# Hybrid attention block: second score pass on half the array's rows for two heads at once, and two pieces of elementwise work issued later

## Chip, cores and metric

One NeuronCore of one Trainium2 chip runs the whole program in one launch. The metric is device time in microseconds (us); the figure before is the median of three runs. TensorE (PE) multiplies matrices, and its weight loads are listed apart as PEld. VectorE is DVE, ScalarE is ACT, GpSimd is POOL, and SyncE (SP) issues the DMAs.

## The reference, cut to what matters

The block has 1024 tokens of width 1024. A gated linear recurrence and a sparse attention run on the same normed input, are merged by gates, and a squared-ReLU MLP follows. The parts that matter here:

```python
qg = q.reshape(...) * (HD ** -0.5)                # 8 heads of 64, in 2 groups of 4
p_s = masked_softmax(einsum('bghqd,bgqkd->bghqk', qb, k_sel), tok_ok)      # selected branch
p_w = masked_softmax(einsum('bghqd,bgkd->bghqk', qb, k_w), m_w)            # window branch
...
hn = rmsnorm(h, norm2_g[l])
h = h + jnp.square(jax.nn.relu(hn @ w_ff1[l])) @ w_ff2[l]
return rmsnorm(h, final_g)
```

With 1024 tokens the selection takes every causal block, so the selected branch is plain causal attention over all keys up to the query. The window branch sees the last 512 keys. A block of 128 queries is called `qb` (0 to 7), a group of four heads `g`.

## The kernel before, in words

**Precision.** Every fp32 matrix is split into a high part (rounded to the engine's fp32r format) and a low rest; a product of two such matrices is three matmuls (high-high, high-low, low-high; `mm3`, L241). For the attention scores the split is laid along the rows instead: a head has 64 channels, so the 128 rows of the array hold q-high in rows 0 to 63 and q-low in rows 64 to 127 (`split_q` L799, transposed into `qS`). The keys in `kS` hold, for x=0, k-high twice (once for each half of the rows) and, for x=1, k-low twice. So one head's scores are two matmuls over all 128 rows (L894): first pass (q-high + q-low) times k-high, second pass (q-high + q-low) times k-low. A mask is added in PSUM by a bf16 matmul of the identity with a 128x128 mask tile (L897): `diag` on the query's own block, `far` on the block four back in the window branch.

**Scores.** `scores(qb, g)` (L851) is a generator that issues one chunk between two `yield`s. A chunk is one PSUM tile of 1024 columns from `psA` (two buffers of two banks). For qb below 4 the tile holds two heads of up to 512 columns (`pair = 2`), for qb 4 to 7 one head of up to 1024 columns. Keys are taken in two halves of 512, because an output lies in one bank. After the matmuls DVE takes the row maximum (L901), ACT the exponential (L910), and after all four heads of a branch DVE the reciprocal (L915) and POOL the scaling (L919).

**Attention.** `attend()` (L1001) walks a list of steps, one for each key block of each branch of each unit (qb, g): four transposes of probabilities on PE into a `psB` bank (L934), a high copy on ACT (L936), a low rest on DVE (L937), and three steps later two matmuls with the values (L1045). Between steps it draws chunks of the scores of the next unit, spread evenly over the steps of the present one (`n_all`, L1020: eight chunks, four where qb is below 4, and one more for the compressed branch when g is 0). The compressed branch's steps have 63 keys, so their two value matmuls use 63 of the array's rows (`vcS`). The tile framework adds the waits and may place an instruction before an earlier one on its engine.

**Second norm.** In the second half of the tokens (th=1), after each of four output tiles j of the merge projection is added to the residual (L1399), the generator `norm2` (L1116) is advanced twice: once for the norm of tile j (h_d DMA, ACT square, POOL power at L249 and L250, DVE scaling at L1122), and once for the tile's sums and differences (L1134 DVE, L1135 POOL, L1136 DVE, L1137 POOL), which the fast (Strassen-like, seven products) MLP needs as operands S1, S2 and S4. After tile 2, `ahead(-1)` prepares the first four MLP weight operands (ACT copy L1185, DVE rest L1186). The MLP's first products P1 need only the first half's A11; S2 and S3 are transposed (L1108, `turned`) after the first and second of them.

**First MLP product.** For each of 16 column pairs p, `f1_prod` (L1203) issues the seven products in the order P1, P6, P7, P2, P5, P4, P3 (12 matmuls each, L1217) into the banks a, c, d, a, e, d, e; c and e are the two halves of one `psA` tile `f1c`. After each product come its sums (`add` is L1221 whatever it adds), ReLU on ACT and square. After P4: `ub[0]` is squared, POOL adds `ud` to it into `ub[1]` (L1253), then DVE subtracts `ua` from `ub[0]` in place (L1254), and a DMA stores `ub`. After P3 the same for `uc` (POOL square L1225, DVE add L1221, DVE L1261, DMA L1262). P6's sum is `u2 = c + p1`, named `u` in the rows. POOL also makes the weight sums `w1t` (L1175) and DVE the rests of the weight operands `w1op` (L1186). On SP's queue the loads of `w1r` (L1167) for p+2 follow the stores of p.

Of the kernel before, what the change touches and what calls it, by code (L numbers as in the profile page):

```python
# [19 lines left out]
D = 1024  # L20
# [5 lines left out]
NH = 8  # L26
# [23 lines left out]
def fb(ap):  # L50
    return ap.bitcast(F32)
# [3 lines left out]
def tile_hybrid_block(ctx, tc, x, positions, norm1_g, w_in, lb_param, hgrn_norm_g, pe_k, pe_v,  # L55
# [733 lines left out]
    def prep(th):  # L789
        qt = QT[th]  # L790
        qS[th] = [a8("qS") for _ in range(2)]
        kS[th] = [a8("kS") for _ in range(2)]
        tmp = s4(name="rtmp")
        for i in range(2):
            rope2(qt[i].rearrange("p t (h d) -> p t h d", h=NH), th, i, NH, tmp[:, i * 256:256 + i * 256])
            yield 1300.0 * th
        QX = {}

        def split_q(h2):  # L799
            qx = QX[h2] = s4(F32R, name="qx").rearrange("p (h t x d) -> p h t x d", h=2, t=4, x=2)  # L800
            for i in range(2):
                src = qt[i].rearrange("p t (h d) -> p h t d", h=NH)[:, h2:h2 + 2]
                hi = qx[:, :, 2 * i:2 * i + 2, 0, :]
                nc.scalar.copy(hi, src)
                nc.vector.tensor_tensor(qx[:, :, 2 * i:2 * i + 2, 1, :], src, fb(hi), op=OP.subtract)

        for br in range(2):
            for g in range(2):
                kx = KXS.pop((th, br, g))
                for x_ in range(2):  # L810
                    pt = psB("ptk")
                    for j in range(4):
                        nc.tensor.transpose(pt[:, j * 128:(j + 1) * 128],
                                            kx[:, j, x_].rearrange("p e d -> p (e d)"), ident)
                    dst = kS[th][br][:, g * 2 + x_, :]
                    if x_:
                        nc.scalar.copy(dst, pt)
                    else:
                        nc.vector.tensor_copy(dst, pt)
                if br:  # L820
                    split_q(g * 2)
                yield 800.0
        for h2 in range(0, NH, 2):
            qx = QX.pop(h2)
            for e in range(2):
                h = h2 + e
                pt = psB("ptq")
                for j in range(4):
                    nc.tensor.transpose(pt[:, j * 128:(j + 1) * 128],
                                        fb(qx[:, e, j]).rearrange("p x d -> p (x d)"), ident)  # L830
                dst = qS[th][h // 4][:, h % 4, :]
                if h % 2:
                    nc.scalar.mul(dst, pt, 0.125)
                else:
                    nc.vector.tensor_scalar(dst, pt, 0.125, None, op0=OP.mult)
            if h2 + 4 < NH:
                split_q(h2 + 4)
            yield 800.0
        del QT[th]
# [11 lines left out]
    def scores(qb, g):  # L851
# [23 lines left out]
            PC[qb] = Pc  # L875
            yield
        den = small.tile([128, 3, 8], F32, name="den", tag="den", bufs=3)
        pair = 2 if qb < 4 else 1
        for br, kb0 in ((0, 0), (1, k_lo)):
            nk = (qb + 1 - kb0) * 128  # L880
            for h0 in range(0, 4, pair):
                sc = psA("sc")
                for hh in range(h0, h0 + pair):
                    off = (hh - h0) * 512
                    for half in range(2):
                        a, e = max(kb0, half * 4), min(qb + 1, half * 4 + 4)
                        if a >= e:
                            continue
                        cs = slice(off + a * 128, off + e * 128)
                        ks = slice((a % 4) * 128, (a % 4 + e - a) * 128)  # L890
                        masks = [(k, m) for k, m in ((qb, diag), (qb - 4, far))
                                 if a <= k < e and (m is diag or br == 1)]
                        for x_ in range(2):
                            nc.tensor.matmul(sc[:, cs], qS[th][g][:, hh, qsl], kS[half][br][:, g * 2 + x_, ks],  # L894
                                             start=x_ == 0, stop=x_ == 1 and not masks)
                        for mi, (k, m) in enumerate(masks):
                            nc.tensor.matmul(sc[:, off + k * 128:off + (k + 1) * 128], identb, m, start=False,  # L897
                                             stop=mi == len(masks) - 1)
                i0 = br * 4 + h0
                sv = sc.rearrange("p (h k) -> p h k", h=pair)[:, :, kb0 * 128:(qb + 1) * 128]  # L900
                nc.vector.tensor_reduce(den[:, 2, i0:i0 + pair], sv, axis=AX.X, op=OP.max, negate=True)  # L901
                for hh in range(h0, h0 + pair):
                    i = br * 4 + hh
                    if qb < 4:
                        if br == 0:
                            PP[qb, g, 8 + hh] = s4(name="P")
                        PP[qb, g, i] = PP[qb, g, 8 + hh][:, br * 512:br * 512 + nk]
                    else:
                        PP[qb, g, i] = s4(name="P")[:, :nk]
                    nc.scalar.activation(PP[qb, g, i], sv[:, hh - h0], AF.Exp, bias=den[:, 2, i:i + 1],  # L910
                                         accum_out=den[:, 0, i:i + 1])
                if h0 + pair == 4:
                    bs = slice(br * 4, br * 4 + 4)
                    nc.vector.tensor_scalar(den[:, 1, bs], den[:, 0, bs], 1e-30, None, op0=OP.max)
                    nc.vector.reciprocal(den[:, 1, bs], den[:, 1, bs])  # L915
                    for h_ in range(4):
                        i = br * 4 + h_
                        pv_ = PP[qb, g, i]
                        nc.gpsimd.tensor_scalar(pv_, pv_, den[:, 1, i:i + 1],  # L919
                                                gat[:, qb, (g * 4 + h_) * 3 + 1 + br:(g * 4 + h_) * 3 + 2 + br],  # L920
                                                op0=OP.mult, op1=OP.mult)
                yield
# [78 lines left out]
    def attend():  # L1001
# [4 lines left out]
        for si in range(len(steps) + LAG):  # L1006
            if si < len(steps):
                qb, g, br, k, i, n = steps[si]
                u = units.index((qb, g))
                if i == 0 and si:  # L1010
                    for _ in nxt:
                        yield 1300.0
                    if u + 1 < len(units):
# [3 lines left out]
                            W.stop = 10 ** 9  # L1017
                            W.ensure(n_before_merge + 1, 0)
                        nb, ng = units[u + 1]
                        nxt, n_done, n_all = scores(nb, ng), 0, (4 if nb < 4 else 8) + (ng == 0)  # L1020
                    else:
                        nxt = iter(())
                        W.stop, W.load, W.ahead = 10 ** 9, 1, 1
# [90 lines left out]
        nc.vector.tensor_tensor(l, p3, fb(h), op=OP.subtract)  # L1114

    def norm2(th, hs_):  # L1116
        for j in range(4):
            t = th * 4 + j
            nc.sync.dma_start(h_d[t * 128:(t + 1) * 128, :], hs_[j])
            hn = HN[t] = s4(name="hn")  # L1120
            rs = rms_scale(hs_[j], hn, D)
            nc.vector.scalar_tensor_tensor(hn, hs_[j], rs, g2b, op0=OP.mult, op1=OP.mult)  # L1122
            yield 2600.0
            if th == 0:
                for q, nm in enumerate(("A11", "A12")):
                    turned(nm, [HN[x_][:, q * 512:(q + 1) * 512] if x_ == j else None for x_ in range(4)], j)
                yield 1000.0
                continue

            if j % 2 == 0:  # L1130
                HS1.append(s4(name="hs1"))
            a11, a12, a21, a22 = HN[j][:, :512], HN[j][:, 512:], hn[:, :512], hn[:, 512:]
            s1 = HS1[j // 2][:, (j % 2) * 512:(j % 2) * 512 + 512]
            nc.vector.tensor_tensor(s1, a21, a22, op=OP.add)  # L1134
            nc.gpsimd.tensor_tensor(a21, a11, a21, op=OP.subtract)  # L1135
            nc.vector.tensor_tensor(a11, s1, a11, op=OP.subtract)  # L1136
            nc.gpsimd.tensor_tensor(a12, a12, a11, op=OP.subtract)  # L1137
            yield 1000.0

    def turn(nm, banks):  # L1140
        x0, c0 = {"S1": (None, 0), "S2": (0, 0), "S3": (4, 0), "S4": (0, 512), "A22": (4, 512)}[nm]
# [61 lines left out]
    def f1_prod(p, nm):  # L1203
# [44 lines left out]
        elif nm == "P4":  # L1248
# [2 lines left out]
            add(ub[:, 0], ps_["d"], post["u2"])  # L1251
            sq(ub[:, 0], nc.vector)
            nc.gpsimd.tensor_tensor(ub[:, 1], ub[:, 0], ud, op=OP.add)  # L1253
            nc.vector.tensor_tensor(ub[:, 0], ub[:, 0], post["ua"][:, 0], op=OP.subtract)  # L1254
            nc.sync.dma_start(u_d[p][2:4].rearrange("x p c -> p x c"), ub)
        else:
            uc = ring("uc", 2, p).rearrange("p (x c) -> p x c", x=2)
            add(uc[:, 0], ps_["e"], post["u2"])
            sq(uc[:, 0], nc.gpsimd)
            add(uc[:, 1], post["ua"][:, 0], uc[:, 0])  # L1260
            nc.vector.tensor_tensor(uc[:, 0], uc[:, 0], post["ud"], op=OP.subtract)  # L1261
            nc.sync.dma_start(u_d[p][4:6].rearrange("x p c -> p x c"), uc)  # L1262
            del UP[p], PB[p]


# [102 lines left out]
    for th in range(2):  # L1368
# [11 lines left out]
        for dh in range(2):  # L1380
# [8 lines left out]
            for j in range(4):  # L1389
# [10 lines left out]
                if th == 1 and dh == 1:  # L1400
                    next(n21)
                    if j == 2:
                        ahead(-1)
                    next(n21)
                pump(2600)
            del ws
        del M[th]
        if th == 0:
            n2 = spawn(norm2(0, hs_))
        else:  # L1410
            ahead(0)
            hs_ = None
    yb = None
# [62 lines left out]
```

## Time and profile before

| what | value |
|---|---|
| median of 3 runs | 1645.74 us (1644.25 to 1648.33) |
| profiled execution | 1644.42 us, its span 1642.7 us, mean granted clock 0.997 |
| PE busy | 1604.9 us (98%), 8342 matmuls |
| PE weight loads | 1338.5 us (81%) |
| DVE busy | 1033.1 us (63%) |
| ACT busy | 740.9 us (45%) |
| POOL busy | 589.2 us (36%) |

A span is the time from the first to the last instruction. An instruction's busy time runs from its start to its end, and successive matmuls overlap, so "busy" is not a count of useful cycles. Attention lies from about 540 to 870 us of the span, the second norm from 977 to 1006 us, the first MLP product from 993 to about 1320 us.

### The profile page before, as it was taken

Reading aid. Unit: us, or ns where it says so; the run is one execution under the profiler, and the core shown is the slowest. Engines: PE = TensorE matmul, PEld = TensorE weight load, DVE = VectorE, ACT = ScalarE, POOL = GpSimd, SP = SyncE. Lnnn points to the kernel's source line nnn. Section 1 sums busy time; section 2 is a strip of 40 time slices with the busy share of each in tenths; the row PEclk is TensorE's granted clock in tenths of the full one; section 3 lists DMA queues with packets and bytes.
Section 4 is the critical chain, followed back from the end, with each engine's and each line's share of the span. In section 5 each row is a group of like instructions: output and inputs, shape, how many; then the busy total and the mean of one; then the engine's idle time right before and its main releaser. Section 6 shows DMA issues by size and latency. Waiting matters only on the chain. (4 is left out here: it accounts for less than half of the span.)

```text
span 1642.7 us, 22944 instructions
## 1 busy us (share of the span) xinstructions
PE 1604.9 (98%) x8342; PEld 1338.5 (81%) x8342; DVE 1033.1 (63%) x1615; ACT 740.9 (45%) x1422; POOL 589.2 (36%) x587
## 2 busy tenths in 40 slices
PE   8999999999999999999999998999999999999998
PEld 7898897889888888788788876877777788888886
DVE  6464454122537467988886646766666678887766
ACT  5343334220646365877764414333333356334443
POOL 2221222010112363444322135455555422564554
PEclk9999999999999999999999999999999999999999
DMA  5210111232434000000037722444444499888852
GB/s 187 72 43 23 39 39 29 85 107 77 132 107 153 27 1 1 1 1 1 14 118 267 269 85 69 141 148 141 141 141 141 167 324 345 305 301 320 301 182 107
DMA packets 145827, 211.67 MB, mean 129 GB/s; under 512 B 11649, under 2 KB 72241, under 8 KB 145714
## 3 DMA queue, kind: packets, MB, share of 16 engines
q1 hardware_dynamic: 145714, 210.21, 38.0%
q8 instruction: 66, 1.08, 0.3%
q14 instruction: 47, 0.39, 0.1%
HBM read 164.03 MB, written 46.14 MB: 128 GB/s over the span
## 5 line engine op out<-in xcount | busy, mean ns | idle before, releaser
L1305 POOL TENSOR_TENSOR gr<-gw 128x512 f32<-128x512 f32 x80 | 124.2, 1565 | 135.2 <-DMA gw<-in_w_ff_dram 72.6
L155 POOL TENSOR_TENSOR wlo<-wraw,whi 128x1024 fp32r<-128x1024 f32 (+1 forms) x28 | 67.4, 2407 | 274.5 <-ACT whi L152 247.2
L242 PE MATMUL gT<-xh,whi 128*128 128x512 f32 x384 | 152.7, 398 | 0.0
L244 PE MATMUL gT<-xh,wlo 128*128 128x512 f32 x384 | 150.3, 391 | 0.0
L243 PE MATMUL gT<-xl,whi 128*128 128x512 f32 x384 | 150.1, 391 | 0.0
L919 POOL TENSOR_SCALAR P<-P,den,gat 128x640 f32<-128x640 f32 (+7 forms) x128 | 100.1, 797 | 120.2 <-DVE den L915 61.3
L155 DVE TENSOR_TENSOR wlo<-wraw,whi 128x1024 fp32r<-128x1024 f32 (+2 forms) x59 | 81.8, 1394 | 94.0 <-ACT whi L152 89.6
L1217 PE MATMUL f1c<-xoh,w1op 128*128 128x512 f32 x384 | 127.8, 394 | 9.3 <-DVE u L1221 9.3
L1186 DVE TENSOR_TENSOR gu<-gr,gu 128x512 fp32r<-128x512 f32 x112 | 103.5, 924 | 47.2 <-ACT gu L1185 47.1
L1185 ACT CAST gu<-gr 128x512 fp32r<-128x512 f32 x112 | 69.4, 620 | 139.6 <-DVE gx L1186 109.7
L1186 DVE TENSOR_TENSOR gx<-gr,gx 128x512 fp32r<-128x512 f32 x112 | 109.7, 980 | 4.0 <-ACT gx L1185 4.0
L937 DVE TENSOR_TENSOR pth<-pT,pth 128x512 fp32r<-128x512 f32 (+1 forms) x148 | 98.7, 682 | 21.3 <-ACT pth L936 19.9
L910 ACT ACTIVATE P<-sc,den 128x640 f32<-128x640 f32 (+7 forms) x128 | 89.7, 705 | 43.9 <-DVE den L901 38.9
L894 PE MATMUL sc<-kS,qS 128*128 128x512 f32 (+3 forms) x384 | 96.7, 361 | 0.6 <-ACT P L910 0.5
L1045 PE MATMUL oT<-pth,vS 128*128 128x512 f32 x264 | 96.7, 441 | 0.0
L936 ACT CAST pth<-pT 128x512 fp32r<-128x512 f32 (+1 forms) x148 | 85.0, 588 | 23.9 <-PE pT L934 19.8
L1217 PEld LDWEIGHTS f1c<-xoh,w1op 128*128 128x128 f32 x384 | 72.0, 188 | 29.1 <-DVE u L1221 13.2
L901 DVE TENSOR_REDUCE den<-sc 128x1 f32<-128x640 f32 (+7 forms) x96 | 84.5, 883 | 16.7 <-PE sc L897 15.9
L152 ACT CAST whi<-wraw 128x1024 fp32r<-128x1024 f32 (+2 forms) x87 | 88.6, 1039 | 12.6 <-PE po L243 6.1
L1217 PE MATMUL f1a<-xoh,w1op 128*128 128x512 f32 x256 | 86.5, 398 | 1.6 <-DVE w1op L1186 1.6
L243 PE MATMUL gA<-gx,gu 128*128 128x512 f32 x224 | 87.4, 390 | 0.4 <-DVE gx L1186 0.2
L242 PE MATMUL gA<-gx,gu 128*128 128x512 f32 x224 | 87.3, 390 | 0.0
(343 smaller groups left out, 4428.6 us busy)
## 6 DMA issues: line engine op xcount, KB each, us to landing
gw<-in_w_ff_dram SPq DMA_DIRECT2D x160, 256.0 KB, 5.3
gr<-u_d SPq DMA_DIRECT2D x112, 256.0 KB, 5.0
wraw<-in_w_in_dram SPq DMA_DIRECT2D x40, 512.0 KB, 5.4
w1r<-in_w_ff_dram SPq DMA_DIRECT2D x32, 512.0 KB, 4.6
wraw<-in_w_out_dram SPq DMA_DIRECT2D x16, 512.0 KB, 6.8
u_d<-ua SPq DMA_DIRECT2D x16, 512.0 KB, 2.8
u_d<-ub SPq DMA_DIRECT2D x16, 512.0 KB, 2.8
u_d<-uc SPq DMA_DIRECT2D x16, 512.0 KB, 3.1
```

The costliest lines, as they stand in the source:

```text
L155: eng.tensor_tensor(lo, raw, fb(hi), op=OP.subtract)
L242: nc.tensor.matmul(o, l[0], r[0], start=start, stop=False)
L243: nc.tensor.matmul(o, l[0], r[1], start=False, stop=False)
L244: nc.tensor.matmul(o, l[1], r[0], start=False, stop=stop)
L894: nc.tensor.matmul(sc[:, cs], qS[th][g][:, hh, qsl], kS[half][br][:, g * 2 + x_, ks], start=x_ == 0, stop=x_ == 1 and not masks)
L910: nc.scalar.activation(PP[qb, g, i], sv[:, hh - h0], AF.Exp, bias=den[:, 2, i:i + 1], accum_out=den[:, 0, i:i + 1])
L919: nc.gpsimd.tensor_scalar(pv_, pv_, den[:, 1, i:i + 1], gat[:, qb, (g * 4 + h_) * 3 + 1 + br:(g * 4 + h_) * 3 + 2 + br], op0=OP.mult, op1= ...
L937: nc.vector.tensor_tensor(pth[:n, 1], pt[:n], fb(pth[:n, 0]), op=OP.subtract)
L1045: nc.tensor.matmul(oT, vv, pth[:m, x_], start=i == 0 and x_ == 0, stop=i == n - 1 and x_ == 1)
L1186: nc.vector.tensor_tensor(l, src, fb(h), op=OP.subtract)
L1217: nc.tensor.matmul(dst, w_[:, kt, :], x_.kt(kt), start=first and kt == 0 and i == 0, stop=kt == 3 and i == 2, skip_group_check=True)
L1305: nc.gpsimd.tensor_tensor(t0[:, 1], t1[:, 0], t1[:, 1], op=OP.add if GORDER[i][1][2] > 0 else OP.subtract)
```

## The change

Four edits:

1. `split_q` writes, for the odd head of a pair, q-high into rows 64 to 127 and q-low into rows 0 to 63, by four half-size pairs of copy and subtraction instead of two.
2. `scores` handles two heads in every chunk. The first pass is as before. The second pass multiplies only q-high with k-low, on 64 rows: the even head on rows 0 to 63, the odd head on rows 64 to 127, one right after the other, into different banks. For qb 4 to 7 a chunk now takes both `psA` tiles, one for each head. The masks of both heads follow the second pass of the half that they are in. The product of q-low and k-low is left out. `n_all` falls from 8 to 4 chunks for qb 4 to 7.
3. `norm2` for the second half of the tokens is advanced once for each tile j instead of twice: the call issues the differences of tile j-2 (from tile 2 on) and then the norm of tile j. The differences of the last two tiles come after the loop (`drain_gen`), before `ahead(0)`.
4. The subtraction `ub[0] -= ua[0]` and the store of `ub` move from after P4 to after P3, behind the store of `uc`.

```diff
             for i in range(2):
-                src = qt[i].rearrange("p t (h d) -> p h t d", h=NH)[:, h2:h2 + 2]
-                hi = qx[:, :, 2 * i:2 * i + 2, 0, :]
-                nc.scalar.copy(hi, src)
-                nc.vector.tensor_tensor(qx[:, :, 2 * i:2 * i + 2, 1, :], src, fb(hi), op=OP.subtract)
+                for e in range(2):
+                    src = qt[i].rearrange("p t (h d) -> p h t d", h=NH)[:, h2 + e]
+                    hi = qx[:, e, 2 * i:2 * i + 2, e, :]
+                    nc.scalar.copy(hi, src)
+                    nc.vector.tensor_tensor(qx[:, e, 2 * i:2 * i + 2, 1 - e, :], src, fb(hi), op=OP.subtract)
...
-        pair = 2 if qb < 4 else 1
...
+            for h0 in (0, 2):
+                if qb < 4:
+                    sc = psA("sc")
+                    scs = [sc[:, :512], sc[:, 512:]]
+                else:
+                    scs = [psA("sc") for _ in range(2)]
+                for x_ in range(2):
                     for half in range(2):
...
+                        for d_ in range(2):
+                            rows = slice(d_ * 64, d_ * 64 + 64) if x_ else slice(0, 128)
+                            nc.tensor.matmul(scs[d_][:, a * 128:e * 128], qS[th][g][rows, h0 + d_, qsl],
+                                             kS[half][br][rows, g * 2 + x_, ks], start=x_ == 0,
+                                             stop=x_ == 1 and not masks)
+                        for d_ in range(2 if x_ else 0):
+                            for mi, (k, m) in enumerate(masks):
+                                nc.tensor.matmul(scs[d_][:, k * 128:(k + 1) * 128], identb, m, start=False,
+                                                 stop=mi == len(masks) - 1)
...
-                        nxt, n_done, n_all = scores(nb, ng), 0, (4 if nb < 4 else 8) + (ng == 0)
+                        nxt, n_done, n_all = scores(nb, ng), 0, 4 + (ng == 0)
...
     def norm2(th, hs_):
-        for j in range(4):
+        for j in range(5):
+            if j < 4:
...
+                yield 2600.0
...
+            if j == 0:
+                continue
+            i = j - 1
...
             nc.vector.tensor_tensor(s1, a21, a22, op=OP.add)
             nc.gpsimd.tensor_tensor(a21, a11, a21, op=OP.subtract)
             nc.vector.tensor_tensor(a11, s1, a11, op=OP.subtract)
             nc.gpsimd.tensor_tensor(a12, a12, a11, op=OP.subtract)
-            yield 1000.0
...
             nc.gpsimd.tensor_tensor(ub[:, 1], ub[:, 0], ud, op=OP.add)
-            nc.vector.tensor_tensor(ub[:, 0], ub[:, 0], post["ua"][:, 0], op=OP.subtract)
-            nc.sync.dma_start(u_d[p][2:4].rearrange("x p c -> p x c"), ub)
         else:
...
             nc.sync.dma_start(u_d[p][4:6].rearrange("x p c -> p x c"), uc)
+            nc.vector.tensor_tensor(ub[:, 0], ub[:, 0], post["ua"][:, 0], op=OP.subtract)
+            nc.sync.dma_start(u_d[p][2:4].rearrange("x p c -> p x c"), ub)
...
                     if j == 2:
                         ahead(-1)
-                    next(n21)
...
+            drain_gen(n21)
             ahead(0)
```

## Rows read from the trace of the kernel before

**Rows 1.** Busy time by stage, 650 to 700 us; columns as in its first line.
```profile
core 0: us, PE busy (x) PEld busy (x) DVE busy (x) ACT busy (x) POOL busy (x), PEclk, DMA share, GB/s
650.00:700.00 50.00, 49.24 (x326) 38.75 (x324) 45.57 (x84) 39.36 (x93) 21.19 (x26) 1.00 0.00 1
```

**Rows 2.** Waits of PE: who waited for whom, us in total, times, longest.
```profile
PE f1c L1217 <- DVE u L1221: 9.3, 12, 0.9
...
PE pt L1108 <- DVE xol L1114: 3.9, 1, 3.9
...
PE f1a L1217 <- DVE w1op L1186: 1.6, 1, 1.6
```

**Rows 3.** Groups by line and shape, PE, score matmuls: busy us, mean ns of one.
```profile
L894 PE MATMUL sc<-kS,qS 128*128 128x512 f32 x144 | 49.1, 429 | 0.6 <-ACT P L910 0.5
...
L894 PE MATMUL sc<-kS,qS 128*128 128x384 f32 x80 | 22.5, 370 | 0.0
...
L894 PE MATMUL sc<-kS,qS 128*128 128x256 f32 x80 | 17.8, 312 | 0.0
...
L894 PE MATMUL sc<-kS,qS 128*128 128x128 f32 x80 | 14.6, 278 | 0.0
```

**Rows 4.** Chain that ended last, in order of time: start us, us, what.
```profile
1202.53 3.03 PE f1c L1217 x12
1205.57 2.73 PE f1d L1217 x12
```

**Rows 5.** Timeline of PE around a compressed-branch step: start us, us, what, count.
```profile
781.73 0.23 PE L897 MATMUL sc<-diag,identb 128*128 128x128 bf16 x1
781.89 0.73 PE L1045 MATMUL oT<-pth,vcS 63*128 63x512 f32 x2
782.55 1.08 PE L894 MATMUL sc<-kS,qS 128*128 128x512 f32 x4
783.47 0.23 PE L897 MATMUL sc<-diag,identb 128*128 128x128 bf16 x1
783.51 0.95 PE L1045 MATMUL oT<-pth,vS 128*128 128x512 f32 x3
```

**Rows 6.** Weight loads of 63 rows: durations (min/median/max ns), and one pair in the timeline.
```profile
L1045 PEld LDWEIGHTS oT<-pth,vcS x32: 182/184/187, 589.4 to 842.7; 63*128 63x128 f32 x32
...
781.89 0.29 PEld L1045 LDWEIGHTS oT<-pth,vcS 63*128 63x128 f32 x2
```

**Rows 7.** Groups by line and shape, 540 to 870 us, DVE and ACT.
```profile
L901 DVE TENSOR_REDUCE den<-sc 128x1 f32<-128x640 f32 x40 | 32.7, 818 | 6.3 <-PE sc L897 5.5
...
L910 ACT ACTIVATE P<-sc,den 128x640 f32<-128x640 f32 x40 | 32.0, 799 | 15.4 <-DVE den L901 12.8 <-POOL P L919 1.7 <-DVE den L915 0.6
...
L804 ACT CAST qx<-qt 128x256 fp32r<-128x256 f32 x16 | 5.8, 422 | 1.8 <-DVE qt L754 1.8
```

**Rows 8.** Timeline of PE inside one head's scores.
```profile
728.30 0.34 PE L894 MATMUL sc<-kS,qS 128*128 128x384 f32 x1
728.48 0.60 PE L934 MATMUL pT<-ident,P 128*128 128x128 f32 x4
```

**Rows 9.** Timelines of DVE, POOL and SP in one column pair of the MLP.
```profile
1216.10 0.69 DVE L1254 TENSOR_TENSOR ub<-ub,ua 128x512 f32<-128x512 f32 x1 [4.79 <-POOL ub L1253]
...
1220.41 0.69 DVE L1221 TENSOR_TENSOR uc<-ua,uc 128x512 f32<-128x512 f32 x1 [2.41 <-POOL uc L1225]
...
1222.22 0.68 DVE L1221 TENSOR_TENSOR u<-f1c,p 128x512 f32<-128x512 f32 x1
...
1218.08 1.30 POOL L1175 TENSOR_TENSOR w1t<-w1r 128x512 f32<-128x512 f32 x1 [2.00 <-DVE w1op L1186]
...
1223.53 1.57 SPq L1167 DMA_DIRECT2D w1r<-in_w_ff_dram  x2
```

**Rows 10.** Timelines of DVE and POOL at the second norm, and the stage behind it.
```profile
1001.75 1.28 DVE L1122 SCALAR_TENSOR_TENSOR hn<-hx,st,grow 128x1024 f32<-128x1024 f32 x1 [2.31 <-POOL st L250]
...
999.52 1.29 POOL L1137 TENSOR_TENSOR hn<-hn 128x512 f32<-128x512 f32 x1 [0.81 <-DVE hn L1136]
...
1005.00:1010.00 5.00, 5.00 (x16) 4.17 (x17) 4.38 (x6) 1.18 (x2) 4.20 (x4) 0.50 0.00 0
```

More of the change, by code (lines that the diff above doesn't have):

```diff
@@ L877, in scores @@
         den = small.tile([128, 3, 8], F32, name="den", tag="den", bufs=3)
-        pair = 2 if qb < 4 else 1
         for br, kb0 in ((0, 0), (1, k_lo)):
             nk = (qb + 1 - kb0) * 128
[L881 to L884, printed above, removed]
+            for h0 in (0, 2):
[5 more added lines that the diff above has]
+                for x_ in range(2):
                     for half in range(2):
@@ L888, in scores @@
                             continue
-                        cs = slice(off + a * 128, off + e * 128)
-                        ks = slice((a % 4) * 128, (a % 4 + e - a) * 128)
                         masks = [(k, m) for k, m in ((qb, diag), (qb - 4, far))
                                  if a <= k < e and (m is diag or br == 1)]
-                        for x_ in range(2):
-                            nc.tensor.matmul(sc[:, cs], qS[th][g][:, hh, qsl], kS[half][br][:, g * 2 + x_, ks],
-                                             start=x_ == 0, stop=x_ == 1 and not masks)
@@ L896, in scores @@
-                        for mi, (k, m) in enumerate(masks):
-                            nc.tensor.matmul(sc[:, off + k * 128:off + (k + 1) * 128], identb, m, start=False,
-                                             stop=mi == len(masks) - 1)
-                i0 = br * 4 + h0
-                sv = sc.rearrange("p (h k) -> p h k", h=pair)[:, :, kb0 * 128:(qb + 1) * 128]
-                nc.vector.tensor_reduce(den[:, 2, i0:i0 + pair], sv, axis=AX.X, op=OP.max, negate=True)
-                for hh in range(h0, h0 + pair):
+                        ks = slice((a % 4) * 128, (a % 4 + e - a) * 128)
@@ new lines, in scores @@
+                i0 = br * 4 + h0
+                ksl = slice(kb0 * 128, (qb + 1) * 128)
+                if qb < 4:
+                    sv = sc.rearrange("p (h k) -> p h k", h=2)[:, :, ksl]
+                    nc.vector.tensor_reduce(den[:, 2, i0:i0 + 2], sv, axis=AX.X, op=OP.max, negate=True)
+                else:
+                    for d_ in range(2):
+                        nc.vector.tensor_reduce(den[:, 2, i0 + d_:i0 + d_ + 1], scs[d_][:, ksl], axis=AX.X,
+                                                op=OP.max, negate=True)
@@ L903, in scores @@
+                for hh in range(h0, h0 + 2):
                     i = br * 4 + hh
@@ L909, in scores @@
                         PP[qb, g, i] = s4(name="P")[:, :nk]
-                    nc.scalar.activation(PP[qb, g, i], sv[:, hh - h0], AF.Exp, bias=den[:, 2, i:i + 1],
+                    nc.scalar.activation(PP[qb, g, i], scs[hh - h0][:, ksl], AF.Exp, bias=den[:, 2, i:i + 1],
                                          accum_out=den[:, 0, i:i + 1])
-                if h0 + pair == 4:
+                if h0 == 2:
                     bs = slice(br * 4, br * 4 + 4)
@@ L1116, in norm2 @@
     def norm2(th, hs_):
-        for j in range(4):
[L1118 to L1123, printed above, removed]
+        for j in range(5):
+            if j < 4:
+                t = th * 4 + j
+                nc.sync.dma_start(h_d[t * 128:(t + 1) * 128, :], hs_[j])
+                hn = HN[t] = s4(name="hn")
+                rs = rms_scale(hs_[j], hn, D)
+                nc.vector.scalar_tensor_tensor(hn, hs_[j], rs, g2b, op0=OP.mult, op1=OP.mult)
+                yield 2600.0
             if th == 0:
-                for q, nm in enumerate(("A11", "A12")):
-                    turned(nm, [HN[x_][:, q * 512:(q + 1) * 512] if x_ == j else None for x_ in range(4)], j)
-                yield 1000.0
+                if j < 4:
+                    for q, nm in enumerate(("A11", "A12")):
+                        turned(nm, [HN[x_][:, q * 512:(q + 1) * 512] if x_ == j else None for x_ in range(4)], j)
+                    yield 1000.0
                 continue
-            if j % 2 == 0:
+            if j == 0:
+                continue
+            i = j - 1
+            if i % 2 == 0:
                 HS1.append(s4(name="hs1"))
-            a11, a12, a21, a22 = HN[j][:, :512], HN[j][:, 512:], hn[:, :512], hn[:, 512:]
-            s1 = HS1[j // 2][:, (j % 2) * 512:(j % 2) * 512 + 512]
+            hm = HN[4 + i]
+            a11, a12, a21, a22 = HN[i][:, :512], HN[i][:, 512:], hm[:, :512], hm[:, 512:]
+            s1 = HS1[i // 2][:, (i % 2) * 512:(i % 2) * 512 + 512]
             nc.vector.tensor_tensor(s1, a21, a22, op=OP.add)
@@ L1137, in norm2, with drain_gen @@
             nc.gpsimd.tensor_tensor(a12, a12, a11, op=OP.subtract)
-            yield 1000.0
+    def drain_gen(g):
+        for _ in g:
+            pass
     def turn(nm, banks):
@@ L1253, in f1_prod @@
             nc.gpsimd.tensor_tensor(ub[:, 1], ub[:, 0], ud, op=OP.add)
-            nc.vector.tensor_tensor(ub[:, 0], ub[:, 0], post["ua"][:, 0], op=OP.subtract)
-            nc.sync.dma_start(u_d[p][2:4].rearrange("x p c -> p x c"), ub)
         else:
+            ub = post["ub"]
             uc = ring("uc", 2, p).rearrange("p (x c) -> p x c", x=2)
```

## The prediction

> **What bounds the kernel now.** I read the busy time by stage first. In the attention stage PE is busy 49.24 of 50 us while DVE has 45.57 and ACT 39.36 [rows 1], and the score matmuls waited 0.6 us in all [rows 3]: there every nanosecond of PE's sequence counts, and DVE is a close second. The waits of PE come next: they say where PE is not the bound. Three of them touch this change: the MLP's first product waits 9.3 us, in 12 pieces, for DVE's `u`, and the start of the MLP waits 3.9 us for a transposed operand's rest and 1.6 us for a weight operand's [rows 2]. So the change has two sorts of parts: edits 1 and 2 alter PE's own sequence where it is full, edits 3 and 4 alter what PE waits for.
>
> **Second score pass.** A 512-column matmul in a stream costs 0.227 us (12 in 2.73 us [rows 4]). The shorter shapes last 58 ns less for every 128 columns [rows 3], so 384 columns cost 0.17 and 256 cost 0.117. Two weight loads of 0.184 us each fill 0.29 us together [rows 6], so one follows the other by 0.11, and a 128-column matmul, which needs a new load, costs that 0.11. Half of the score matmuls are second passes: 72, 40, 40 and 40 [rows 3]; side by side they are 36, 20, 20 and 20 pairs.
>
> *The price of 64 rows.* The trace shows it at the compressed branch's value matmuls, which use 63 rows [rows 5]. The two end at 782.62, 0.66 us after the mask before them ended (781.96). Three full-height ones behind a mask end 0.76 after it (783.70 to 784.46), so two take 0.53: going in costs 0.13 behind a mask. There the next load shows already (0.53 against 2 x 0.227), by 0.08, so it is 0.2 behind another matmul. The four score matmuls that follow end at 783.63, 1.01 after the 63-row pair, where 2 x 0.227 + 2 x 0.17 = 0.79 would do: coming out costs 0.22. I take 0.20 each way. Of this 0.11 is the weight load that can't be made beforehand. Each chunk goes in and out once: 8 query blocks x 2 groups x 2 branches x 2 pairs = 64 stays. For qb 4 to 7 the window branch's `far` mask, a full-height matmul, splits a stay in two: 16 more, 80 in all. Every stay ends in a mask, whose load no row shows apart; coming out into a mask lies between 0.09 (nothing of a load shows) and 0.20, and I take 0.09 because the mask itself lasts 0.23 at most with its load [rows 5].
>
> *The sum.* Going in: 64 x 0.20 + 16 x 0.13 = +14.9. Where the first piece has 128 columns (16 stays) its load shows before too: -0.8. Coming out: 80 x 0.09 = +7.2. Masks now stand in twos, so one of the two exposed loads behind them goes: 80 x 0.05 = -4.0 (0.08 behind long pieces, nothing behind short ones). A pair side by side: I take the second matmul to start one weight load, 0.11, behind the first, so a pair saves 0.227 - 0.11, 0.17 - 0.11 and nothing for the shortest two: 36 x 0.117 + 20 x 0.06 = -5.4. The 16 stays with two pieces pay that offset once: 16 x 0.11 = -1.8. Together **+10.1 us**, all of it on PE in a full stage. The bounds: nothing side by side takes back the last two terms, +17.3, and coming out at 0.20 adds 8.8, +26. Loads that cost a pair nothing save the whole of a second matmul: 36 x 0.227 + 20 x 0.17 + 20 x 0.117 + 20 x 0.11 = 16.1 in place of 7.2, +1.2. I take the middle since the only loads of this height follow each other by 0.11 [rows 6], though they share their rows. By the Trainium skill ("TensorE: Matmul & The Clock Gate", Part 3, "The mechanism") matmuls in distinct row groups start some 4 ns apart; by that the sum would be the +1.2. No row here shows two row groups at once.
>
> *DVE, ACT, POOL and SP.* Maxima, exponentials and scalings keep number and size. `split_q` turns 16 ACT copies of 0.422 us [rows 7] into 32 of half size; if a half cost as much as a whole it is 6.8 us, half of it in 650 to 700 us, where ACT idles 10.6 us [rows 1], and DVE's 16 rests likewise, against 4.4 us idle there: priced at nothing, and at up to 2 us if that cover is gone. No DMA is touched.
>
> **The moved subtraction.** In a column pair DVE stands 4.79 us before `ub`'s subtraction, because POOL still reads `ub`; behind it stand `uc`'s sum and a weight rest, which POOL waits for with `w1t` (2.00 idle); then DVE waits 2.41 for POOL's square of `uc`, and only then makes `u` (1222.22), for which PE waits [rows 9]. Moved behind `uc`, the subtraction blocks nobody: `uc`'s sum and the rest can run from 1211.3, POOL goes on 2.00 earlier, and `u` comes 2.00 earlier less the 0.6 us of the subtraction that now stands in front of it: it ends at about 1221.5. PE needs it at 1202.53 + 7 x 2.73 = 1221.6 [rows 4]. So the wait goes, with 0.1 us to spare. A wait also costs the start-up of the next block, 3.03 against 2.73 [rows 4]: 9.3 + 12 x 0.30 = 12.9 us. On SP the store of `ub` now stands behind that of `uc` and before the loads of `w1r` [rows 9]; these wait anyway for a weight rest that DVE makes behind `u`, so they move with `u`, earlier. Bounds: nothing (the wait comes back in another place) to 12.9; with so little to spare I take **-11.5**.
>
> **The second norm.** The last tile's scaling on DVE waited 2.31 us for POOL's `st`, which stood behind the previous tile's difference L1137 (999.52, 1.29 us) [rows 10]; behind that scaling stood the rest `xol` that PE waited 3.9 us for [rows 2]. PE then ran at half clock: 0.50 from 1005 to 1010 [rows 10], the lower of its two levels (1.2 GHz), after that idle time; 5.0 us of work at half rate lose 2.5. The change puts both differences of the last tiles behind the last norm, and the norm of tile 2 before the weight rests has less in front, so the 1.6 should go too: 3.9 + 1.6 + 2.5 = 8.0 at most. But S2's transposes need the differences of tiles 0 and 1, and tile 1's are now issued only at tile 3, behind four weight rests on DVE and the residual's sum: a chain of DVE 0.69, POOL 1.29 and DVE 0.69 [rows 9, 10] that begins about when PE arrives there. That wait of up to 2.7 us is what is late next. Bounds 0 and -8.0; I take **-4.5**. The h_d stores keep their order on SP.
>
> **Sum.** 10.1 - 11.5 - 4.5 = -5.9 us. The profiled execution took 1644.42 us, 1.7 over its span and 1.3 under the median 1645.74; I lay the difference on the median: 1639.8 us. A measurement of this kernel can tell about 0.3%, 4.9 us, from no change.
>
> **Rivals.**
> - *Loads hidden (B).* If the odd head's load runs beside the even head's matmul, attention costs +1.2 and the sum is -14.8: 1631 us. For it: different rows. Against it: loads 0.11 apart [rows 6].
> - *Pairs fall apart (C), slower.* For qb 4 to 7 a chunk takes both score tiles at once. Its two heads now end together; the second tile is free only after 0.82 + 0.82 (two maxima) + 0.80 (one exponential) = 2.4 us at 640 columns [rows 7]. Between chunks PE has, where 9 steps carry 5 chunks, 1.8 steps of 4 x 0.11 + 2 x 0.227 = 0.9 us, 1.6 us in all: short by 0.8. PE's order isn't the code's: transposes stand inside a head's scores [rows 8]. So the first head may go ahead alone, in and out of 64 rows by itself. That costs a further 0.20 + 0.09 and the 0.117 saved, 0.41, in up to 48 stays (16 + 32), 19.7 us. It decides from the point where the second tile comes later than the first head's first pass. At three in four, +14.8: sum +8.9, 1654.6 us. Against it: DVE and ACT have some slack, and longer units have 3.5 steps to a chunk.
> - *The waits return (D).* `u` has 0.1 us to spare. If half of its gain stays away, the sum is -0.2: 1645.6 us. If instead the pairs run one after the other, it is +1.3, 1647 us. Either is a change that can't be told from none; the second is the change not doing what it says.
>
> **Chances.** Forecast 0.40, B 0.18, C 0.22, D 0.20. The forecast lies near the 0.3% line (1640.8), with a range of its own of 1634 to 1644: 0.28 of it falls under faster and 0.12 under same. With B, faster is 0.46; with D and the near edge of C, same is 0.33; slower 0.21. The range runs from 1629, past B, to 1654, most of C: the far ends (+26, or every gain at its bound) stay outside.
>
> **What would show it.** Right: the pair's second weight load 0.11 behind the first and its matmul starting with it; 0.2 us lost at each start of a stay; no wait of PE for `u`, DVE's long stand before the square of `uc` alone; granted clock 1.0 from 1000 to 1010 us. Wrong: second passes of one head standing alone between full-height matmuls (C), pairs that end a full matmul apart (D), or a new PE wait before S2's transposes as long as the two that went.

## The result, and the profile after

The changed kernel takes **1680.1 us** (median; 1678.3 to 1680.7) against 1645.1 of the kernel before on the same chip: a ratio of 1.0215 [1.0201, 1.023], some 35 us slower. The forecast was 1639.8, with a range up to 1654: wrong in sign and size.

The loss is in the attention stage. The score matmuls, by first and last start, before and after:

```profile
L894 PE MATMUL sc<-kS,qS x384: 220/363/499, 570.5 to 837.5; 128*128 128x512 f32 x72, 128*128 128x128 f32 x40, 128*128 128x256 f32 x40, 128*128 128x384 f32 x40
```

```profile
L899 PE MATMUL sc<-kS,qS x384: 217/384/505, 571.0 to 868.7; 128*128 128x512 f32 x48, 64*128 64x512 f32 x48, 128*128 128x256 f32 x18, 64*128 64x256 f32 x18
```

So 267.0 us became 297.7: **+30.7**. The groups by line and shape of the changed kernel (busy us, mean ns of one) answer to [rows 3]:

```profile
L899 PE MATMUL sc<-kS,qS 64*128 64x512 f32 x72 | 30.7, 484 | 0.0
...
L899 PE MATMUL sc<-kS,qS 64*128 64x256 f32 x40 | 10.6, 360 | 0.0
```

Busy time counts overlapping instructions once. Forty 64-row matmuls of 256 columns at 0.360 us would be 14.4 us if none overlapped another, and 7.2 if all stood side by side in pairs. They are 10.6: half of the pairs of this shape don't exist. Over all shapes 34 of the 96 pairs start together in the trace: 29 of 32 in blocks 0 to 3, but 5 of 64 in blocks 4 to 7. The timeline of PE in the window branch of block 6 shows what stands there instead:

```profile
787.01 0.38 PE L899 MATMUL sc<-kS,qS 64*128 64x256 f32 x1
787.33 0.23 PE L904 MATMUL sc<-far,identb 128*128 128x128 bf16 x1
787.49 0.43 PE L899 MATMUL sc<-kS,qS 64*128 64x384 f32 x1
787.86 0.23 PE L904 MATMUL sc<-diag,identb 128*128 128x128 bf16 x1
787.89 0.48 PE L1058 MATMUL oT<-pth,vS 128*128 128x512 f32 x1
...
789.74 0.45 PE L899 MATMUL sc<-kS,qS 64*128 64x384 f32 x1
```

One head's 64-row matmuls stand alone between full-height masks; the other head's follow 2.25 us later, just as alone. In the whole trace PE goes into 64 rows 126 times for scores (two expectations below say 127), where 80 were forecast: 35 in blocks 0 to 3 and 91 in blocks 4 to 7. New waits of PE come with it (560 to 910 us; before they were 1.1 us in all):

```profile
PE oT L1058 <- DVE pth L950: 1.8, 3, 0.7
PE sc L899 <- ACT P L923: 1.5, 3, 0.6
PE py L970 <- DVE oh L959: 0.8, 3, 0.3
PE pT L947 <- DVE pth L950: 0.8, 2, 0.5
```

Of edits 3 and 4 PE's waits show nothing. In the MLP they are those of [rows 2], one 0.8 the more, and the second norm again ends in a stretch at half clock, 1.2 GHz (the second fence, columns as in [rows 1]):

```profile
PE f1c L1239 <- DVE u L1243: 9.8, 12, 0.9
PE pt L1121 <- DVE xol L1127: 3.9, 1, 3.9
...
PE f1a L1239 <- DVE w1op L1208: 1.6, 1, 1.6
PE f1a L1239 <- ACT w1op L1207: 0.8, 1, 0.8
```

```profile
1040.00:1045.00 5.00, 3.88 (x14) 3.32 (x14) 4.15 (x7) 0.78 (x2) 3.67 (x3) 0.50 0.00 0
```

Edit 3 was carried out in part. POOL's last difference of tile 2 now stands behind the last tile's `st`, so the last scaling on DVE waits 0.72 us where it waited 2.31 [rows 10]; the tile's other sum and differences still stand in front of it. But POOL's difference, started 0.07 us earlier, now runs beside the scaling, which takes 2.29 us in place of 1.28. The scaling ends 6.46 us after the start of the residual's last sum (`hx`), where it was 5.83:

```profile
1032.72 0.68 DVE L1422 TENSOR_TENSOR hx<-hx,po 128x512 f32<-128x512 f32 x1
...
1036.89 2.29 DVE L1136 SCALAR_TENSOR_TENSOR hn<-hx,st,grow 128x1024 f32<-128x1024 f32 x1 [0.72 <-POOL st L250]
```

Edit 4 wasn't carried out at all, as DVE's timeline in a column pair shows. The moved subtraction (L1284) still stands **before** `uc`'s sum (its first L1243), though the code now issues it after `uc`'s difference (L1282):

```profile
1252.38 0.69 DVE L1284 TENSOR_TENSOR ub<-ub,ua 128x512 f32<-128x512 f32 x1 [3.54 <-POOL ub L1275]
1252.99 0.69 DVE L1243 TENSOR_TENSOR uc<-f1c,u 128x512 f32<-128x512 f32 x1
...
1256.69 0.69 DVE L1243 TENSOR_TENSOR uc<-ua,uc 128x512 f32<-128x512 f32 x1 [2.41 <-POOL uc L1247]
...
1257.90 0.69 DVE L1282 TENSOR_TENSOR uc<-uc,ud 128x512 f32<-128x512 f32 x1
1258.50 0.68 DVE L1243 TENSOR_TENSOR u<-f1c,p 128x512 f32<-128x512 f32 x1
```

The order on an engine is thus not the order of the code: the framework's scheduler sets it, and it put the subtraction back. It also split the pairs of heads, which the code issues side by side.

### The profile page after: what moved, and what is told of

Same layout as the page of the kernel before. It is cut to its first block, busy times and chain, and to the rows that moved or that the text cites. A ratio compares the mean times of both kernels' runs of the same rounds, so it can differ in the third digit from the quotient of the medians.

```text
span 1679.0 us, 22961 instructions
## 1 busy us (share of the span) xinstructions
PE 1634.1 (97%) x8342; PEld 1338.3 (80%) x8342; DVE 1034.3 (62%) x1631; ACT 741.8 (44%) x1438; POOL 591.5 (35%) x587
## 4 chain that ended last, share of the span: by engine, by line
PE 83%; DVE 6%; POOL 3%; ACT 3%; issue 2%; DMA 1%; SPq 1%; POOLq 0%; ACTq 0%; DVEq 0%
PE f1c L1239 7%; PE gT L244 5%; PE gT L243 5%; PE gT L242 5%; PE sc L899 4%; PE oT L1058 4%; PE pT L947 4%; PE f1a L1239 3%; PE f1d L1239 3%; PE gA L243 3%; PE gA L244 3%; PE gA L242 3%; PE gB L243 3%; PE gB L242 3%; PE gB L244 3%
## 5 line engine op out<-in xcount | busy, mean ns | idle before, releaser
L899 PE MATMUL sc<-kS,qS 64*128 64x512 f32 (+7 forms) x384 | 106.5, 383 | 1.6 <-ACT P L923 1.5
L1208 DVE TENSOR_TENSOR gx<-gr,gx 128x512 fp32r<-128x512 f32 x112 | 105.2, 940 | 3.3 <-ACT gx L1207 2.9
L949 ACT CAST pth<-pT 128x512 fp32r<-128x512 f32 (+1 forms) x148 | 82.2, 592 | 27.3 <-PE pT L947 22.8
L243 PE MATMUL gA<-gx,gu 128*128 128x512 f32 x224 | 87.4, 390 | 0.4 <-DVE gx L1208 0.2
L242 PE MATMUL gA<-gx,gu 128*128 128x512 f32 x224 | 87.3, 390 | 0.0
L244 PE MATMUL gA<-gx,gu 128*128 128x512 f32 x224 | 87.2, 389 | 0.0
```

The costliest lines, as they stand in the source:

```text
L242: nc.tensor.matmul(o, l[0], r[0], start=start, stop=False)
L243: nc.tensor.matmul(o, l[0], r[1], start=False, stop=False)
L244: nc.tensor.matmul(o, l[1], r[0], start=False, stop=stop)
L899: nc.tensor.matmul(scs[d_][:, a * 128:e * 128], qS[th][g][rows, h0 + d_, qsl], kS[half][br][rows, g * 2 + x_, ks], start=x_ == 0, stop=x_ ...
L1208: nc.vector.tensor_tensor(l, src, fb(h), op=OP.subtract)
```

## The experiments

All times are medians; a ratio is to the kernel before on the same chip. "Stage" is the time from the first to the last start of a score matmul, 267.0 us before.

### The two halves of the change

**second_pass** has edits 1 and 2 alone, **orders** edits 3 and 4 alone, each with the change's own lines, as

```diff
+rows = slice(d_ * 64, d_ * 64 + 64) if x_ else slice(0, 128)     # second_pass
```

```diff
-            nc.vector.tensor_tensor(ub[:, 0], ub[:, 0], post["ua"][:, 0], op=OP.subtract)
...
             nc.vector.tensor_tensor(uc[:, 0], uc[:, 0], post["ud"], op=OP.subtract)
...
+            nc.vector.tensor_tensor(ub[:, 0], ub[:, 0], post["ua"][:, 0], op=OP.subtract)   # orders
```

> The second score pass on 64 rows alone (edits 1 and 2 of the change), the subtraction of ub and the second norm as before. Theory: the whole loss is in the attention stage and edits 3 and 4 are worth nothing, so the time is that of the changed kernel within 2 us, 1678 to 1682 us, +33 to +36 on before; PE's 12 waits for u stay at 9 to 10 us. Rival (edits 3 and 4 brought what the prediction said, and the second pass cost that much more): 1692 to 1697 us, with longer waits for u than the changed kernel has.

Measured: 1677.3 us against 1644.1, 1.0198 [1.0183, 1.0213]: +33.2; the stage +32.3.

> The moved subtraction and the second norm alone (edits 3 and 4); the scores as before. Theory (the framework's scheduler puts the moved instructions back to where they stood): within 1.5 us of before, PE's 12 waits for u still 9 to 10 us, xol's 3.9 us still there. Rival, the prediction's: 1630 us, -16, and no wait for u.

Measured: 1645.1 us, 1.0001 [0.9991, 1.001]; PE's waits for `u` 9.1 us in 11. The second pass makes the loss, and edits 3 and 4 together are worth nothing. The subtraction of `ub` didn't move here either, so its reason wasn't put to the test; the second norm stands as in the changed kernel (the last scaling takes 2.28 us after a wait of 0.71).

### The price of 64 rows

**low_pairs** keeps the pairs for blocks 0 to 3, where both heads share one score tile; **heads_alone** adds the 64-row passes of blocks 4 to 7 in the old order, one head after the other.

```diff
+for hh in range(h0, h0 + pair):
+    rows = slice(hh % 2 * 64, hh % 2 * 64 + 64) if x_ and qb < 4 else slice(0, 128)   # low_pairs
+    rows = slice(hh % 2 * 64, hh % 2 * 64 + 64) if x_ else slice(0, 128)              # heads_alone
```

> Before with the pairs of 64 rows for query blocks 0 to 3 alone, where both heads stand in one score tile already; blocks 4 to 7 as before, one head at a time on 128 rows. Theory (the price of a stay was right, the grouping for blocks 4 to 7 is what failed): 32 stays, going in 32 x 0.195 = +6.2, coming out 32 x 0.09 = +2.9, masks in twos -1.6, second matmuls whole beside the first 8 x (0.227 + 0.17 + 0.117 + 0.11) = -5.0, together +2.5, from 0 to +5 us. Rival (a stay costs much more than the rows showed, the rest of the kernel being set back by it): +8 us or more.

> As low_pairs, and blocks 4 to 7 also make the second pass on 64 rows, but one head at a time in the order of before, so nothing stands side by side there and only one score tile is taken at a time. Theory: 96 more stays with nothing saved, 64 x 0.285 + 32 x 0.22 = +25 us on low_pairs, and waits of PE in the attention stage as before (under 2 us): 1668 to 1675 us, so about 5 us less than second_pass, whose pairs fell apart to nearly the same stays but with 5 us of waits. Rival (taking two score tiles at once is no part of the loss): the same as second_pass, 1677 us.

Measured: low_pairs 1647.9 us, 1.0018 [1.0008, 1.0028], +2.8; heads_alone 1672.3, 1.0171 [1.0156, 1.0185], +27.3 and so +24.4 on low_pairs, for 96 stays more (131 against 35): 0.25 us each. Both came as worked out; the interval of low_pairs reaches from 1.3 to 4.6 us above before. The stages, low_pairs first:

```profile
L895 PE MATMUL sc<-kS,qS x384: 218/382/502, 569.1 to 839.6; 128*128 128x512 f32 x88, 128*128 128x128 f32 x24, 128*128 128x256 f32 x24, 128*128 128x384 f32 x24
```

```profile
L895 PE MATMUL sc<-kS,qS x384: 217/388/503, 570.8 to 865.5; 128*128 128x512 f32 x48, 64*128 64x512 f32 x48, 128*128 128x128 f32 x16, 64*128 64x128 f32 x16
```

That is +3.5 and +27.7, with PE waiting no more than before (1.2 and 1.3 us). heads_alone, with one head at a time and the old grouping, shows that the stays, without any new grouping, make +27.3 of second_pass's +33.2. It also answers what the changed kernel's grouping bought: nothing. second_pass is slower by 4.6 us of stage, and has 3.6 us more of waits and two windows of 50 us at a mean granted clock of 0.97.

In low_pairs 29 of the 32 pairs hold. Their two matmuls start 3 to 4 ns apart. Sixteen matmuls of 0.381 us are 6.1, and they fill 3.1:

```profile
L895 PE MATMUL sc<-kS,qS 64*128 64x256 f32 x16 | 3.1, 381 | 0.0
```

### Grouping without 64 rows, and pairs by force

**full_rows** keeps the new grouping on full height; **pairs_kept** fixes each 64-row matmul behind its predecessor in the code.

```diff
-rows = slice(d_ * 64, d_ * 64 + 64) if x_ else slice(0, 128)
+rows = slice(0, 128)                                              # full_rows
```

```diff
-nc.tensor.matmul(scs[d_][:, a * 128:e * 128], ...
+mm_ = nc.tensor.matmul(scs[d_][:, a * 128:e * 128], ...
+if x_:
+    tc.keep_in_program_order(mm_)                                 # pairs_kept
```

> As second_pass, but each second pass runs on all 128 rows, as before (so the product of the two rests is in again): the new grouping of heads and chunks without a change of height. Theory (the loss is the change of height, paid in more than 127 stays, of which the pairs that fall apart are a part): the attention stage costs -4 to +8 us against before, 1642 to 1653 us. Rival (the loss is the new grouping: two score tiles taken at once, waits for them, DVE and ACT in another order): +15 us or more, 1660 us or over.

> As second_pass, with every 64-row score matmul fixed behind the matmul that the code issues before it, so that the pairs of query blocks 4 to 7 too stand side by side. Theory (pairs that fell apart are the larger part of the loss): 80 stays of 64 rows in place of 127, and 0.41 us less for each of 47, some 19 us; with loads that cost a pair nothing another 5 us less: 1655 us, and up to 1665 if PE waits for the second score tile take the place. Rival (the switches themselves cost it all, 80 stays as much as 127): over 1672 us.

Measured: full_rows 1657.2 us, 1.0076 [1.0061, 1.0091], +13.1, a miss for both numbers but nearer the rival; its stage is 9.9 longer. PE's waits there:

```profile
PE sc L899 <- ACT P L923: 4.0, 7, 1.3
PE oT L1058 <- DVE pth L950: 2.2, 3, 0.9
PE oT L1058 <- ACT pth L949: 1.2, 1, 1.2
PE py L970 <- DVE oh L959: 1.2, 3, 0.5
```

With two small ones they come to 9.4 us, 8.3 more than before: the new grouping costs this much in waits by itself. Of it 3.5 us is for the exponential (`P`) that frees a score tile; most of the rest is for the copies and rests of the probabilities (`pth`).

pairs_kept: 1680.8 us, 1.022 [1.0203, 1.0238]. A miss: the time lies where the rival put it, but not for the rival's reason. The pairs hold (91 of 96 start together, in 85 stays), and nothing is won. One of its shapes, its longest group of waits, and two windows of the stage (columns as in [rows 1]):

```profile
L899 PE MATMUL sc<-kS,qS 64*128 64x256 f32 x40 | 7.3, 359 | 0.0
```

```profile
PE sc L899 <- ACT P L925: 13.7, 27, 1.4
```

```profile
700.00:750.00 50.00, 46.31 (x271) 33.46 (x270) 35.39 (x61) 29.54 (x65) 18.69 (x21) 0.93 0.00 1
...
800.00:850.00 50.00, 46.37 (x260) 33.15 (x257) 35.38 (x58) 28.37 (x58) 16.54 (x17) 0.90 0.04 11
```

Every pair of this shape is there (7.3 us for 40 x 0.359), but PE waits 27 times for a score tile, 15.4 us with the other waits, 14.3 more than before. Behind such waits the granted clock falls to its lower level, 1.2 GHz, in four stretches, 17.1 us together, which costs at most 3.5 + 5.0 us in these windows. If each wait costs a start-up of 0.30 as in [rows 4], that is 8.1 more. Of the stage's +33.4 in this execution, the longest of the four (1684.8 us), that leaves some 2.5 us for the switches themselves. This last split is an estimate, since its parts can overlap; the waits and the clock are rows.

### The moved subtraction, made to move

**pinned** takes orders and fixes the subtraction of `ub` behind `uc`'s difference, and the differences of tiles 2 and 3 of the norm in code order; **pinned_sub** fixes the subtraction alone.

```diff
-nc.vector.tensor_tensor(ub[:, 0], ub[:, 0], post["ua"][:, 0], op=OP.subtract)
+tc.keep_in_program_order(
+    nc.vector.tensor_tensor(ub[:, 0], ub[:, 0], post["ua"][:, 0], op=OP.subtract))
...
+pin = tc.keep_in_program_order if i > 1 else (lambda ins: ins)    # pinned only
+pin(nc.vector.tensor_tensor(s1, a21, a22, op=OP.add))             # and the other three alike
```

> The moved subtraction and the second norm alone (as in orders), with the subtraction of ub fixed on DVE behind the difference of uc, and the differences of the tiles 2 and 3 of the second norm fixed in the order of the code on DVE and POOL. Theory (the reasons for edits 3 and 4 were right and the framework's scheduler undid them): PE's 12 waits for u fall under 2 us, -8 to -12.9, and of the xol wait and the half clock up to -8: 1626 to 1637 us. Rival (the wait comes back elsewhere: in u, in the weight rests behind the fixed subtraction): 1641 us or over, waits of PE in the MLP's first part still 9 us or more in sum.

> As pinned, but only the subtraction of ub is fixed; the second norm is left to the scheduler. Theory: the waits for u go, those for xol and the half clock behind it stay: 1632 to 1637 us. Rival: no gain, as orders. The difference to pinned is what the order of the second norm is worth: 0 to 8 us by the prediction.

Measured: pinned 1634.8 us, 0.9936 [0.9924, 0.9948]; pinned_sub 1635.6, 0.9937 [0.9924, 0.9949]. Both are some 10 us faster than before, and level with each other: fixing the order of the second norm's last differences brings nothing that these runs can tell.

The trace of pinned shows why. The last scaling now comes 2.81 us after the residual's last sum (before: 4.55, from 997.20 to 1001.75 [rows 10]), and it lasts 1.28, so that part worked. But the differences of tiles 2 and 3, fixed behind it, are late, and PE waits for a bank whose `xol` stands behind them:

```profile
999.88 0.68 DVE L1411 TENSOR_TENSOR hx<-hx,po 128x512 f32<-128x512 f32 x1
1002.69 1.28 DVE L1123 SCALAR_TENSOR_TENSOR hn<-hx,st,grow 128x1024 f32<-128x1024 f32 x1 [2.13 <-POOL st L250]
...
1010.49 0.69 DVE L1143 TENSOR_TENSOR hn<-hs,hn 128x512 f32<-128x512 f32 x1 [1.81 <-POOL hn L1142]
1011.09 0.68 DVE L1114 TENSOR_TENSOR xol<-pt,xoh 128x512 fp32r<-128x512 f32 x1
```

```profile
1008.82 0.63 PE L1108 MATMUL pt<-ident,hn 128*128 128x128 f32 x4 [1.48 <-DVE xol L1114]
...
1011.83 0.66 PE L1108 MATMUL pt<-ident,hn 128*128 128x128 f32 x4 [1.45 <-DVE xol L1114]
```

One wait of 3.9 us became three, 3.5 in all, and the wait of 1.6 us for a weight operand stayed.

### The subtraction alone, and a smaller edit of the norm

**sub_only** is the kernel before with only the fixed subtraction. **sub_late** also puts POOL's last difference of the last tile but one behind the last tile's `st`.

```diff
+            for p_, q_ in late:                                   # behind rms_scale of the next tile
+                tc.keep_in_program_order(nc.gpsimd.tensor_tensor(p_, p_, q_, op=OP.subtract))
...
-            nc.gpsimd.tensor_tensor(a12, a12, a11, op=OP.subtract)
+            if j == 2:
+                late.append((a12, a11))
+            else:
+                nc.gpsimd.tensor_tensor(a12, a12, a11, op=OP.subtract)
```

> Before with the subtraction of ub alone moved and fixed on DVE behind the difference of uc; scores and second norm are those of before. Theory (the moved subtraction is worth what the prediction said once it does move, and the rewritten second norm brought nothing in pinned_sub): 1632 to 1635 us, -10 to -12.9, the best of the kernels so far or level with pinned. Rival (a part of the gain of pinned came from the second norm's code): 1637 us or over.

> As sub_only, and in the second norm only POOL's last difference of the last tile but one is put behind the two st steps of the last tile, so that this difference (1.29 us) no longer stands in front of the last scaling, while all differences that S2's transposes need first stay where they are. Theory (in pinned the gain on the last scaling was eaten by transposes that waited for the delayed differences of the first tiles): the last scaling comes up to 1.3 us earlier and the xol wait of 3.9 us shrinks by as much, 0 to -2.5 us on sub_only with less time at half clock. Rival (the wait is for the weight rests or the tile's own chain): no change in the xol wait.

Measured: sub_only **1633.0 us**, 0.9932 [0.9915, 0.9948], 11.4 us faster than the 1644.3 beside it; sub_late 1632.8, 0.9936 [0.9922, 0.995]. They can't be told apart. sub_only, with one moved subtraction and its store, is the simplest version that beats both kernels. PE's waits at `f1c`, 9.3 us before, and DVE's order:

```profile
PE f1c L1217 <- ACT w1op L1185: 0.6, 1, 0.6
PE f1c L1217 <- DVE u L1221: 0.6, 2, 0.3
```

```profile
1250.55 0.69 DVE L1221 TENSOR_TENSOR uc<-ua,uc 128x512 f32<-128x512 f32 x1 [4.68 <-POOL uc L1225]
1251.27 0.69 DVE L1259 TENSOR_TENSOR uc<-uc,ud 128x512 f32<-128x512 f32 x1
1251.88 0.68 DVE L1263 TENSOR_TENSOR ub<-ub,ua 128x512 f32<-128x512 f32 x1
...
1253.09 0.69 DVE L1221 TENSOR_TENSOR u<-f1c,p 128x512 f32<-128x512 f32 x1
```

DVE's two stands of 4.79 and 2.41 us [rows 9] are one of 4.68, and `u` comes in time.

In sub_late the last scaling waits 0.71 us for POOL where it waited 2.31 [rows 10], but it takes longer itself; its rows on DVE and on POOL:

```profile
1001.46 2.31 DVE L1127 SCALAR_TENSOR_TENSOR hn<-hx,st,grow 128x1024 f32<-128x1024 f32 x1 [0.71 <-POOL st L250]
```

```profile
1001.39 1.29 POOL L1125 TENSOR_TENSOR hn<-hn 128x512 f32<-128x512 f32 x1
```

The `xol` wait shrank from 3.8 to 3.2 us in its trace, too little to show in the time. On DVE and POOL this is what edit 3 did in the changed kernel. (The expectation of sub_late puts pinned's waits down to the differences of the first tiles; the rows above are of tiles 2 and 3.)

## Why the prediction was wrong, and where it was right

- **The step that failed first: the second pass, +10.1, measured +33.2.** Its prices of a stay held: going in, coming out and the masks, tried where no chunk takes two tiles, gave +2.8 and +24.4 where +2.5 and +25 were worked out. What failed is the count: 80 stays in pairs were assumed, and 126 came, since in blocks 4 to 7 only 5 of 64 pairs stood together. That is what rival C forecast, and where. It got 0.22 because DVE and ACT "have some slack" and longer units more steps; that argument was wrong. Its reason, a late second tile, fits the runs: full_rows waits for score tiles on full height too (4.0 us, before 0.5), and in pairs_kept, where the pairs are held, PE waits 27 times for `P`. That the scheduler split the pairs for this reason is not shown. Rival C was also priced too low, at three in four of its 48 further stays (46 came) and without the waits.
- **One term had the wrong value but little weight.** The second matmul of a pair was put 0.11 us behind the first. In low_pairs it starts 3 to 4 ns behind, and sixteen matmuls fill the time of eight: it costs nothing visible, the lower bound of that term. With it the prediction's own sum is +1.2, so by these prices the second pass would have had nothing to win even with every pair in place. By the Trainium skill ("TensorE: Matmul & The Clock Gate", Part 3, "The mechanism") the offset is some 4 ns; low_pairs agrees, with its 3 to 4. The row on which 0.11 rested [rows 6] is of loads that share their rows, and doesn't bear on this.
- **The moved subtraction, -11.5, measured nothing, because it did not move.** The prediction took the code's order for DVE's, though it noted of PE that "PE's order isn't the code's" [rows 8]. Once fixed in place it brought 11.4 us (sub_only), by the mechanism that was worked out: the `f1c` wait for `u` falls from 9.3 to 0.6.
- **The second norm, -4.5, measured nothing: what it won on one wait it lost beside it.** Of the differences of the last two tiles only POOL's last one of tile 2 moved in the changed kernel. The last scaling's wait fell by 1.59 us, and the scaling itself grew by 1.01. With the last differences fixed in the code's order (pinned) the scaling is early and short, but PE waits 3.5 us behind the differences of tiles 2 and 3 in place of 3.9. The prediction named a wait of that sort as "late next", but for tile 1's differences; those were done by 995 us, before the last scaling began. The wait of 1.6 us for a weight operand, which the prediction let go, stayed at 1.6 in every trace. The bound of 0 should have been the value.
- **`split_q`'s doubled copies** were priced at nothing. Nothing in low_pairs, which has them, asks for more: its +2.8 is level with the 2.5 of the switches.
- "The change not doing what it says" stood among the rivals only for the pairs, as loads that don't overlap. That the moved instructions might not move was not considered.

Three things stay open: why the scheduler split the pairs, whether they would pay with more score tiles (not tried; the +1.2 speaks against it), and how the cost in pairs_kept divides between waits, clock and start-ups.

## What to carry to other kernels

Before pricing a reordered instruction, read in the trace whether the engine follows the code's order at all; where a scheduler sets it, an edit of the order alone may be no edit, and the move must be fixed in place (here 0 against 11.4 us). Price a mode of the array by the number of times that it is entered and left, and ask what must hold for the entries to be shared: a pair that needs two free buffers at once is only as cheap as the second buffer is early. Take the saving of a pair and the wait for its buffer as one term, since forcing the one brings the other.

## What the runs showed of the hardware

- Matmuls on the two halves of the rows really run side by side: 16 of 0.381 us in 3.1 us (low_pairs), with no price for the second that a row shows.
- Entering and leaving 64 rows costs 0.25 us a stay here (24.4 us for 96), more than a whole 512-column matmul in a stream (0.227 [rows 4]), which is the most that one pair in the stay can save. In low_pairs a stay holds one pair, and it is 2.8 us slower than before. That several pairs in one stay would pay is an estimate from these numbers; no run tried it.
- DVE's scaling, which reads two operands from SBUF, took 2.31 us with POOL's difference started 0.07 us before it (sub_late), and 1.28 alone [rows 10]; POOL's took its usual 1.29. Taking POOL's work out of the wait and putting it beside the scaling gave most of the gain back. By the Trainium skill ("SBUF — State Buffer", "SBUF: two separate sides"), where a DVE instruction with two SBUF inputs meets a POOL one that reads SBUF, the one that starts later is blocked until the other's instruction ends. POOL's had 1.22 us to go, and DVE's lost 1.03: the rows agree with the direction and come near the size.
- The granted clock fell to 1.2 GHz in four stretches of pairs_kept's score stage, each behind waits of PE for `P`; the two windows above, with PE busy 46.3 and 46.4 of 50 us, so have means of 0.93 and 0.90. In pairs_kept itself from 750 to 800 us, with 45.8 busy, and in full_rows, with 47.4 to 48.5 (650 to 850 us), it stayed at 2.4 GHz: idle time came before each fall, but didn't always bring one.
